# Kept sums of weights made in DRAM by adding transfers instead of on VectorE

## The chip, the cores and the metric

One core of one Trainium2 chip. The time is the device time of one execution in microseconds, the median of some runs. A core has five engines that run their own instruction streams in order and wait for each other through semaphores: TensorE (PE; its weight loads are shown as PEld), VectorE (DVE), ScalarE (ACT), GpSimd (POOL) and SyncE (SP), which here only issues transfers. 16 DMA engines serve the transfers that SP, ACT and POOL issue.

## The reference

Two layers over 256 tokens of width 2048, float32. Layer 0 mixes tokens by neighbourhood attention (16 heads), layer 1 by a gated short convolution; each is followed by a gated MLP (width 5632) with a convolution over three positions. Cut to what matters:

```python
for i in range(2):
    a = rms_norm(h, mix_norm[i])
    mixed = (neighborhood_attention(a, na_w_qkv[0], na_rpb[0], na_w_o[0]) if i == 0 else
             short_conv_mixer(a, sc_w_in[0], sc_conv_w[0], sc_w_out[0]))
    h = h + mixed
    h = h + conv_glu_ffn(rms_norm(h, ffn_norm[i]), ffn_w_up[i], ffn_conv_w[i], ffn_conv_b[i], ffn_w_down[i])
return rms_norm(h, final_norm)
# conv_glu_ffn: [g, u] = dwconv3(x @ w_up) + b;  (silu(g) * u) @ w_down
```

## The kernel before

Every float32 matrix product is split: a weight tile (`raw`, one chunk of 8 x 128 columns, 512 KB) is cast by ScalarE to a short part `hi` (line 185), VectorE subtracts to get the rest `lo` (line 188), and TensorE multiplies hi x both parts of the activations and lo x their high part. There are six `raw`, six `hi` and six `lo` buffers; SP may load a chunk when the subtraction that read the buffer's old content is over.

Two kinds of products follow each other. A `Phase` (QK, up projections, short-conv input; lines 262 and 270) gives features on partitions; an item of it is two output tiles of four chunks in all. `Tokens` (attention output, down projections, short-conv output; lines 463 to 465) gives tokens on partitions. For certain pairs of contraction tiles, marked H in the plans, `Tokens` uses a Strassen-like form with seven products in place of eight (`seven`, line 467). It needs sums of weight blocks. With l, r and t for the left block, the right block of the same rows and the right block of the next, these are l+r, t+r and l+r+t, 256 KB each. They are made long before, while another product runs, and kept in DRAM: this is the "kept" tensor, one per marked pair and half of the columns, 64 in all. One such making is a job.

The job is written by `make`. It takes three tiles of the activation pool (`act_tile`), loads l, r and t into them through SP, and puts off two steps in the list `stores`: ADDS chunks later VectorE does three adds (lines 207 to 209), and STORES chunks later ScalarE issues three stores (line 214). `take` hands jobs to phases; a phase gives its jobs to the items from `hosts[0]` to `hosts[1]`. QK_JOBS, V_JOBS, UP_JOBS and SC_JOBS say how many jobs which phase gets: none in the last head group of the attention, 11, 10, 8 and 10 in the four up projections, 15 in the short-conv input.

The seven products need sums of activation blocks as well, the forms: `make_forms` adds them on GpSimd (lines 526 to 529) from two finished `conv` tiles, and `split_into` (lines 301 and 302, ScalarE and VectorE) splits them in two parts at once.

The order of instructions on each engine is fixed when the program is built, by a scheduler that follows the program's order and `issue_after` edges. `tick` counts places in an item's run; `after(n, fn)` puts a step off by n ticks.

In the attention, four head groups alternate between a `Phase` for queries and keys and `Values` (lines 689 to 691). Scores, softmax and its transposes are strewn into them: VectorE scales the scores and adds the bias (line 624; GpSimd added a mask to the bias before, line 603), finds the maximum (627) and, after the exponential on ScalarE (629), normalises (632); TensorE transposes the result (642) into a PSUM tile that has one buffer, and ScalarE and VectorE split that (301, 302).

Of the kernel before, what the change touches and what calls it, by code (L numbers as in the profile page):

```python
# [15 lines left out]
F32 = mybir.dt.float32  # L16
F32R = mybir.dt.float32r
AF = mybir.ActivationFunctionType
ALU = mybir.AluOpType
# [3 lines left out]
P = 128  # L23
# [35 lines left out]
QK_JOBS, V_JOBS, UP_JOBS, SC_JOBS = (0, 2, 2, 0), (2, 2, 2, 0), (11, 10, 8, 10), 15  # L59
# [12 lines left out]
C_END = C_ID + P  # L72

LEAD = 96
ADDS, STORES = 1, 3
RAWS = 6


# [1 line left out]
def trunk(ctx, tc, xT, par, bias, wqk, wv, wo, wsc, wscout, wup, wdown, out):  # L80
    nc = tc.nc
# [48 lines left out]
    def prep_to(n):  # L130
        while len(prepped) < min(n, len(chunks)):
            src, w, kind = chunks[len(prepped)]
            for due in [x for x in stores if x[0] <= len(prepped)]:
                stores.remove(due)
                due[1]()
            if kind == "make":
                make(*src)
                prepped.append(())
                continue
            raw = wp.tile([P, CH * P], F32, name="raw", tag="raw", bufs=RAWS)  # L140
            if kind == "rows":
                load(raw[:, :w], src)
                prepped.append(parts(raw[:, :w]) + (raw,))
                continue

            if kind == "kept":
                t42, left, sums = prepped[-1][2], prepped[-2][2], src()
                load(t42[:, 4 * P:], sums[:, 8 * P:])
                load(raw, sums[:, :8 * P])
                nc.vector.tensor_add(out=t42[:, :4 * P].rearrange("p (f c) -> p f c", f=4),  # L150
                                     in0=t42[:, 4 * P:].rearrange("p (f c) -> p f c", f=4),
                                     in1=left.rearrange("p (f k c) -> p k f c", f=4, c=P)[:, 1])
                prepped.append((parts(raw), parts(t42)))
                continue

            load(raw[:, :4 * w].rearrange("p (f c) -> p f c", f=4), src.rearrange("f p c -> p f c"))
            prepped.append(parts(raw[:, :4 * w].rearrange("p (f k c) -> p f k c", f=4, c=P)) + (raw,))

    def load(out, in_, strict=True):

        with ExitStack() as order:
            if "SP" in newest:
                order.enter_context(tc.issue_after(newest["SP"].ins))
            last = nc.sync.dma_start(out=out, in_=in_)
        if strict:
            newest["SP"] = last
# [23 lines left out]

    kept, newest, fenced = {}, {}, []

    def make(w, g, i, sets, strict):

        kept[id(w), g, i] = dst = dp.tile([P, 3, 4 * P], F32, name=f"kept{len(kept)}")
        if len(sets) < 2:
            sets.append([act_tile().bitcast(F32) for _ in range(3)])
        else:
            sets.reverse()
        for x, f, k in zip(sets[-1], (0, 4, 4), (0, 0, 1)):  # L200
            f, k = 8 * g + f, 2 * i + k
            load(x.rearrange("p (f c) -> p f c", f=4), w[f:f + 4, :, k * P:(k + 1) * P].rearrange("f p c -> p f c"), strict)
        l, r, t = sets[-1]

        def adds():
            with tc.issue_after(newest["DVE"].ins):
                nc.vector.tensor_add(out=l, in0=l, in1=r)
                nc.vector.tensor_add(out=r, in0=t, in1=r)
                nc.vector.tensor_add(out=t, in0=l, in1=t)

        def store():
            for n, x in enumerate((l, r, t)):
                with tc.issue_after(newest["ACT"].ins):
                    nc.scalar.dma_start(out=dst[:, n], in_=x)
        stores.append((len(prepped) + ADDS, adds))
        stores.append((len(prepped) + STORES, store))

    jobs = []
# [1 line left out]
    def plan_jobs(w, plans):  # L220
        jobs.extend((w, g, i) for g, (order, sset, _) in enumerate(plans) for i in order if i in sset)

    def take(n, strict=True):
        sets = []
        out, jobs[:] = [(*job, sets, strict) for job in jobs[:n]], jobs[n:]
        return out

    class Phase:
# [52 lines left out]
    def after(n, fn):  # L281
        later.append((at[0] + n, fn))

    item = [0]
    at = [0]
# [9 lines left out]
    def split_into(hi, lo, src):  # L295

        with ExitStack() as order:
            if fenced:
                for x in ("ACT", "DVE"):
                    order.enter_context(tc.issue_after(newest[x].ins))  # L300
            first = nc.scalar.copy(out=hi, in_=src)  # L301
            nc.vector.tensor_sub(out=lo, in0=src, in1=hi.bitcast(F32))  # L302
        return first
# [9 lines left out]
    def act_tile():  # L313
        return ap_.tile([P, 2 * S], F32R, name="act", tag="act", bufs=HALF)
# [194 lines left out]
    def form_slots(blocks):  # L509

        if not form_at:
            return [left_over.pop() for _ in range(3)]
        tag = next(x for x in form_at if blocks == 3 or x != "sf")
        form_at.remove(tag)
        y = tp.tile([P, (6 if tag == "sf" else 8) * P], F32R, name="sf", tag=tag)
        if tag != "sf" and blocks == 3:
            left_over.append(y[:, 6 * P:])
        return y

    def make_forms(xe, xo, place, fresh=False):  # L520

        if fresh:
            form_at[:], left_over[:] = ("sf", "vv", "qk") * 2, ()
        v = tp.tile([P, 4, P], F32, name="s", tag="s")
        x11, x21, x12, x22 = (x[:, t * P:(t + 1) * P] for x in (xe, xo) for t in range(2))
        nc.gpsimd.tensor_sub(out=v[:, 0, :], in0=x21, in1=x22)
        nc.gpsimd.tensor_sub(out=v[:, 1, :], in0=v[:, 0, :], in1=x11)
        nc.gpsimd.tensor_add(out=v[:, 3, :], in0=x12, in1=v[:, 1, :])
        nc.gpsimd.tensor_sub(out=v[:, 2, :], in0=x11, in1=x21)  # L529
        if isinstance(place, tuple):  # L530
            hi, lo = place
            split_into(hi, lo, v.rearrange("p f c -> p (f c)"))
            return [(hi[:, j * P:(j + 1) * P], lo[:, j * P:(j + 1) * P]) for j in (0, 1, 3, 2)]

        blocks = 3 if place else 4
        y = form_slots(blocks)
        if isinstance(y, list):
            for j in range(3):
                split_into(y[j][:, :P], y[j][:, P:], v[:, j])
            at = [(x[:, :P], x[:, P:]) for x in y]  # L540
        else:
            y = y.rearrange("p (b t c) -> p t b c", t=2, c=P)
            split_into(y[:, 0, :blocks], y[:, 1, :blocks], v[:, :blocks])
            at = [(y[:, 0, j], y[:, 1, j]) for j in range(blocks)]
        if place:
            at.append((place[:, P:2 * P], place[:, 3 * P:]))
            split_into(*at[3], v[:, 3])
        return [at[j] for j in (0, 1, 3, 2)]

    def in_both(plans, i):  # L550
# [2 lines left out]
    def to_norm(n, a):  # L553

        ssq = ep.tile([P, 2, KT // 4], F32, name=f"ssq{n}")

        def evac(t, q, ps):
            added = residual(t, q, ps)
            squares(t, q, ssq)

            def next_input():
                for k0, tag in zip(range(4 * q - 4, 4 * q + 4, 2), ("tr", "o", "sc", "st")):
                    tr = transposed(k0, tag)
                    for k in range(2):
                        a[k0 + k] = a_tile()
                        scaled_split(a[k0 + k], tr[:, k, :], norm_g(n, k0 + k))
            if t and q % 2:
                after(1, next_input)
                if q == KT // 4 - 1:
                    after(2, lambda: spread_factor(token_factor(ssq)[0]))  # L570
            return added
        return evac


    a0 = [None] * KT
# [284 lines left out]
        plan_jobs(down[1, half], S_MLP[1, half])  # L860
    for g in range(NH // 4):
        Phase(wqk, range(8 * g, 8 * g + 8), KT, a0, qk_evac, intro=0 if g else INTRO, step=STEP,
              jobs=take(QK_JOBS[g], False), hosts=(0, 4))
        Values(g, a0, take(V_JOBS[g], False))
    Tokens(wo, KT, oT, to_norm(1, a1), S_ATT, oforms)
    mlp(0, a1, to_norm(2, a2))
    Phase(wsc, range(3 * KT), KT, a2, sc_evac, intro=3, jobs=take(SC_JOBS), hosts=(8, 29))
# [36 lines left out]
    for r in range(KT // STEP):  # L904
        for i in range(STEP // 2):
            k = r * STEP + 2 * i
# [12 lines left out]
    for item[0], (ph, ft, c, k0, ka, kb) in enumerate(items):  # L919

        with ExitStack() as order:
# [4 lines left out]
            if item[0] != KT // STEP * INTRO:  # L926
# [3 lines left out]
                end, n = ends[item[0]], FURTHER if getattr(ph, "fence", False) else AHEAD  # L930
# [77 lines left out]
```

## Time and profile before

| | before |
|---|---|
| median of 3 runs, us | 2202.33 (2196.28 to 2202.39) |
| profiled execution, us | 2200.65 |
| its span, us | 2198.8 |
| PE, PEld busy, us | 2181.2, 1890.9 |
| DVE, ACT, POOL busy, us | 1847.5, 1305.4, 118.5 |
| three adds of the jobs (L207, L208, L209), us | 44.4, 44.6, 45.5, x64 each |
| stores of the jobs (L214) | 192 of 256 KB, 4.8 us to landing |
| DMA in all | 555.34 MB, mean 253 GB/s |
| HBM read, written | 500.70 MB, 52.43 MB |

Busy times are unions over the span. Matmuls are pipelined and overlap: the mean time of one (391 ns for a 128x512 product) is longer than the distance at which they follow each other. In the tables of windows each row is a stretch of the span; a PE that is busy for the whole stretch at clock 1.00 cannot be made faster by any other engine there.

### The profile page before, as it was taken

The page shows a single profiled execution, that of the slowest core. Times are in us where ns is not written, and L with a number is a line of the kernel's source. Part 1 is how long each engine was busy: PE and PEld are TensorE (multiplying, and loading weights), DVE is VectorE, ACT ScalarE, POOL GpSimd, SP SyncE. Part 2 cuts the span into 40 slices and gives each one's busy share as a digit, 9 for nine tenths or more (in the row PEclk, how much of TensorE's full clock was granted, in tenths as well). Part 3 has the DMA queues.
Part 4 walks back from the last instruction along what each step waited for, and adds up shares of the span by engine and source line. Part 5 has one row for each costly group of instructions (what it writes and reads, how often), then busy time and mean ns, then how long its engine had stood idle before and what let it go on. Part 6 is the DMA issues. An engine that isn't in the chain of part 4 may idle for free.

```text
span 2198.8 us, 33369 instructions
## 1 busy us (share of the span) xinstructions
PE 2181.2 (99%) x11716; PEld 1890.9 (86%) x11716; DVE 1847.5 (84%) x2842; ACT 1305.4 (59%) x1985; POOL 118.5 (5%) x155
## 2 busy tenths in 40 slices
PE   9999999999999999999999999999999999999998
PEld 8888888888888888888888888888888888888886
DVE  8787677888988889988888777888898898898787
ACT  7555556666655656665665555565666665666565
POOL 1010000001100000100000100000010000000000
PEclk9999999999999999999999999999999999999999
DMA  8687656789858879866878888776976787897575
GB/s 302 223 294 229 222 166 212 229 275 315 272 182 268 275 254 317 293 208 216 268 250 290 291 292 291 234 240 221 302 262 198 230 274 253 295 311 242 177 259 173
DMA packets 362072, 555.34 MB, mean 253 GB/s; under 512 B 21680, under 2 KB 249136, under 8 KB 361904
## 3 DMA queue, kind: packets, MB, share of 16 engines
q1 hardware_dynamic: 332880, 502.23, 70.0%
q10 hardware_dynamic: 29024, 50.98, 6.1%
q8 instruction: 92, 1.51, 0.3%
q14 instruction: 76, 0.62, 0.1%
HBM read 500.70 MB, written 52.43 MB: 252 GB/s over the span
## 4 chain that ended last, share of the span: by engine, by line
PE 96%; DVE 1%; DMA 1%; issue 1%; SPq 0%; ACT 0%; DVEq 0%
PE mm L262 42%; PE mm L270 22%; PE mm L465 7%; PE mm L463 7%; PE mm L464 7%; PE mu L463 3%; PE mu L465 3%; PE mu L464 3%; PE mm L690 1%; PE mm L689 1%; PE mm L691 1%; DMA act<-in_wdown 1%; PE tr L371 1%; DMA bias<-in_bias 0%; DVE lo L188 0%
## 5 line engine op out<-in xcount | busy, mean ns | idle before, releaser
L185 ACT CAST hi<-raw 128x1024 fp32r<-128x1024 f32 (+1 forms) x920 | 917.6, 1012 | 372.6 <-PE mm L465 128.6
L188 DVE TENSOR_TENSOR lo<-raw,hi 128x1024 fp32r<-128x1024 f32 (+1 forms) x856 | 1020.1, 1215 | 141.1 <-ACT hi L185 66.1
L262 PE MATMUL mm<-a,hi 128*128 128x512 f32 x4096 | 963.1, 391 | 0.3 <-DVE a L310 0.2
L262 PEld LDWEIGHTS mm<-a,hi 128*128 128x128 f32 x4096 | 758.8, 188 | 152.4 <-DVE a L310 1.3
L270 PEld LDWEIGHTS mm<-a,lo 128*128 128x128 f32 x4096 | 514.0, 191 | 12.5
L270 PE MATMUL mm<-a,lo 128*128 128x256 f32 x4096 | 519.4, 283 | 0.0
L463 PE MATMUL mm<-hi,act 128*128 128x512 f32 x634 | 247.3, 390 | 0.0
L465 PE MATMUL mm<-hi,act 128*128 128x512 f32 x634 | 246.7, 389 | 0.0
L464 PE MATMUL mm<-lo,act 128*128 128x512 f32 x576 | 224.4, 390 | 0.0
L341 DVE SCALAR_TENSOR_TENSOR conv<-pad,pt,conv 128x256 f32<-128x256 f32 x384 | 181.2, 484 | 19.1 <-ACT conv L339 13.4
L325 ACT COPY corr<-mm 128x256 f32<-128x256 f32 x256 | 92.6, 370 | 174.9 <-PE mm L270 171.3
L339 ACT ACTIVATE conv<-pad,pt 128x256 f32<-128x256 f32 x176 | 104.1, 600 | 153.9 <-DVE pad L331 139.4
L465 PEld LDWEIGHTS mm<-hi,act 128*128 128x128 f32 x634 | 119.0, 188 | 24.7
L463 PEld LDWEIGHTS mm<-hi,act 128*128 128x128 f32 x634 | 119.1, 188 | 24.4 <-DVE h L360 0.2
L464 PEld LDWEIGHTS mm<-lo,act 128*128 128x128 f32 x576 | 108.2, 188 | 22.0
L326 DVE TENSOR_TENSOR corr<-mm,corr 128x256 f32<-128x256 f32 x256 | 106.7, 420 | 17.4 <-ACT corr L325 16.6
L529 POOL TENSOR_TENSOR s<-conv 128x128 f32<-128x128 f32 x27 | 29.3, 1085 | 993.5 <-DVE conv L748 993.5
L302 DVE TENSOR_TENSOR act<-conv,act 128x256 fp32r<-128x256 f32 x88 | 39.0, 443 | 48.2 <-ACT act L301 48.0
L331 DVE TENSOR_TENSOR pad<-corr,rstd 128x256 f32<-128x256 f32 x176 | 73.2, 424 | 0.3
L463 PE MATMUL mu<-hi,sf 128*128 128x512 f32 x180 | 70.0, 389 | 0.0
L464 PE MATMUL mu<-lo,sf 128*128 128x512 f32 x180 | 70.0, 389 | 0.0
L465 PE MATMUL mu<-hi,sf 128*128 128x512 f32 x180 | 70.0, 389 | 0.0
(160 smaller groups left out, 1594.1 us busy)
## 6 DMA issues: line engine op xcount, KB each, us to landing
raw<-in_wup SPq DMA_DIRECT2D x352, 512.0 KB, 5.3
raw<-in_wdown SPq DMA_DIRECT2D x124, 512.0 KB, 4.9
kept<-act ACTq DMA_DIRECT2D x192, 256.0 KB, 4.8
raw<-in_wsc SPq DMA_DIRECT2D x96, 512.0 KB, 5.4
act<-in_wdown SPq DMA_DIRECT2D x156, 256.0 KB, 6.0
raw<-kept SPq DMA_DIRECT2D x64, 512.0 KB, 4.9
raw<-in_wqk SPq DMA_DIRECT2D x56, 512.0 KB, 5.4
raw<-in_wv SPq DMA_DIRECT2D x32, 512.0 KB, 4.5
```

The source lines that it names most:

```text
L185: newest["ACT"] = nc.scalar.copy(out=hv, in_=r)
L188: newest["DVE"] = nc.vector.tensor_sub(out=lv, in0=r, in1=hv.bitcast(F32))
L262: nc.tensor.matmul(self.ps[ft], lhsT=prepped[i][0][:, o:o + P], rhs=self.src[k], start=k == 0, stop=False)
L270: nc.tensor.matmul(self.ps[ft][:, S:], lhsT=prepped[i][1][:, o:o + P], rhs=self.src[k][:, :S], start=False, stop=k == self.nk - 1)
L325: nc.scalar.copy(out=corr, in_=ps[:, S:])
L326: nc.vector.tensor_add(out=corr, in0=ps[:, :S], in1=corr)
L331: nc.vector.tensor_mul(out=dst, in0=both(ps), in1=rstd)
L339: nc.scalar.activation(c, x[:, 1:S + 1], AF.Identity, scale=w[1], bias=b)
L341: nc.vector.scalar_tensor_tensor(out=c, in0=x[:, tap:tap + S], scalar=w[tap], in1=c, op0=ALU.mult, op1=ALU.add)
L463: nc.tensor.matmul(ps, lhsT=xh, rhs=wh, start=start, stop=False)
L464: nc.tensor.matmul(ps, lhsT=xh, rhs=wl, start=False, stop=False)
L465: nc.tensor.matmul(ps, lhsT=xl, rhs=wh, start=False, stop=stop)
```

## The change

The three tiles of activations are no longer used by a job. SP copies l, t and t straight into the kept tensor, DRAM to DRAM. After that GpSimd issues transfers that add to what is there (`accum_op`): r to the first piece, r to the second, and, when the first has landed, the first piece to the third. The first two stand ADDS = 2 chunks after the copies, the third STORES = 5 chunks. Neither VectorE nor ScalarE has a part in a job. `strict`, which ordered a job's loads among the others on SP, is gone: all of them are loads that later ones need not follow. And `make_forms` no longer splits at once: where it made its own tiles the splits come LATE = 4 ticks later. Lines from 215 on move up by a few.

```diff
-ADDS, STORES = 1, 3
+ADDS, STORES = 2, 5
+LATE = 4
...
-    def make(w, g, i, sets, strict):
+    def make(w, g, i):
 
         kept[id(w), g, i] = dst = dp.tile([P, 3, 4 * P], F32, name=f"kept{len(kept)}")
-        if len(sets) < 2:
-            sets.append([act_tile().bitcast(F32) for _ in range(3)])
-        else:
-            sets.reverse()
-        for x, f, k in zip(sets[-1], (0, 4, 4), (0, 0, 1)):
-            f, k = 8 * g + f, 2 * i + k
-            load(x.rearrange("p (f c) -> p f c", f=4), w[f:f + 4, :, k * P:(k + 1) * P].rearrange("f p c -> p f c"), strict)
-        l, r, t = sets[-1]
+        l, r, t = (w[8 * g + f:8 * g + f + 4, :, (2 * i + k) * P:(2 * i + k + 1) * P].rearrange("f p c -> p f c")
+                   for f, k in ((0, 0), (4, 0), (4, 1)))
+        at = [dst[:, n].rearrange("p (f c) -> p f c", f=4) for n in range(3)]
+        for n, x in ((0, l), (1, t), (2, t)):
+            load(at[n], x, False)
 
         def adds():
-            with tc.issue_after(newest["DVE"].ins):
-                nc.vector.tensor_add(out=l, in0=l, in1=r)
-                nc.vector.tensor_add(out=r, in0=t, in1=r)
-                nc.vector.tensor_add(out=t, in0=l, in1=t)
+            nc.gpsimd.dma_start(out=at[0], in_=r, accum_op=ALU.add)
+            nc.gpsimd.dma_start(out=at[1], in_=r, accum_op=ALU.add)
 
         def store():
-            for n, x in enumerate((l, r, t)):
-                with tc.issue_after(newest["ACT"].ins):
-                    nc.scalar.dma_start(out=dst[:, n], in_=x)
+            nc.gpsimd.dma_start(out=at[2], in_=at[0], accum_op=ALU.add)
         stores.append((len(prepped) + ADDS, adds))
         stores.append((len(prepped) + STORES, store))
...
-    def take(n, strict=True):
-        sets = []
-        out, jobs[:] = [(*job, sets, strict) for job in jobs[:n]], jobs[n:]
+    def take(n):
+        out, jobs[:] = jobs[:n], jobs[n:]
         return out
...
         if isinstance(y, list):
-            for j in range(3):
-                split_into(y[j][:, :P], y[j][:, P:], v[:, j])
             at = [(x[:, :P], x[:, P:]) for x in y]
+            to = [(*at[j], v[:, j]) for j in range(3)]
         else:
             y = y.rearrange("p (b t c) -> p t b c", t=2, c=P)
-            split_into(y[:, 0, :blocks], y[:, 1, :blocks], v[:, :blocks])
             at = [(y[:, 0, j], y[:, 1, j]) for j in range(blocks)]
+            to = [(y[:, 0, :blocks], y[:, 1, :blocks], v[:, :blocks])]
         if place:
             at.append((place[:, P:2 * P], place[:, 3 * P:]))
-            split_into(*at[3], v[:, 3])
+            to.append((*at[3], v[:, 3]))
+
+        def splits():
+            for x in to:
+                split_into(*x)
+        after(LATE, splits)
```

How the order of instructions moves is shown at three places. The first is VectorE in the values of head group 0, from the scaling of one head's scores (`s_835`, then `s_831`) to the splits of the first transposed tile (`tr_879`, then `tr_866`). Before:

```order
L207 TENSOR_TENSOR act_864<-act_864,act_865 128x512
L302 TENSOR_TENSOR qk_765<-qk_763,qk_765 128x256
L595 TENSOR_TENSOR qk_790<-corr_787,rstd_82 128x256
L208 TENSOR_TENSOR act_865<-act_866,act_865 128x512
L624 SCALAR_TENSOR_TENSOR s_835<-sc_828,bias_624 128x256
...
L302 TENSOR_TENSOR act_884<-tr_879,act_884 128x256
L188 TENSOR_TENSOR lo_905<-raw_902,hi_904 128x1024
L630 RECIPROCAL z_837<-z_837 128x2
L188 TENSOR_TENSOR lo_926<-raw_923,hi_925 128x1024
L632 TENSOR_SCALAR s_835<-s_835,z_837 128x256 x2
L302 TENSOR_TENSOR act_885<-tr_879,act_885 128x256
```

Now:

```order
L189 TENSOR_TENSOR lo_895<-raw_892,hi_894 128x1024
L621 SCALAR_TENSOR_TENSOR s_831<-sc_824,bias_624 128x256
L295 TENSOR_TENSOR qk_765<-qk_790,qk_765 128x256
L621 SCALAR_TENSOR_TENSOR s_831<-sc_824,bias_624 128x256
L295 TENSOR_TENSOR act_871<-tr_866,act_871 128x256
L624 TENSOR_REDUCE m_832<-s_831 128x2
L295 TENSOR_TENSOR act_872<-tr_866,act_872 128x256
```

The adds are gone, and the two splits of the transposed tile stand on both sides of the reduction, with no conversion (`lo`) between them. On TensorE the second set of transposes of this group stands ten products earlier than before; in groups 1 and 2 the transposes keep their places.

The second is VectorE in group 1, between the normalisations of two heads. Before:

```order
L632 TENSOR_SCALAR s_1590<-s_1590,z_1592 128x256 x2
L207 TENSOR_TENSOR act_1637<-act_1637,act_1638 128x512
L188 TENSOR_TENSOR lo_1706<-raw_1703,hi_1705 128x1024
L208 TENSOR_TENSOR act_1638<-act_1639,act_1638 128x512
L207 TENSOR_TENSOR act_1676<-act_1676,act_1677 128x512
L209 TENSOR_TENSOR act_1639<-act_1637,act_1639 128x512
L208 TENSOR_TENSOR act_1677<-act_1678,act_1677 128x512
```

Of these the change keeps the normalisation and the conversion (`lo`); the adds have no successor on VectorE.

The third is GpSimd in the same part, where `bias` is the bias of a head. Before:

```order
L603 TENSOR_TENSOR bias_1293<-bias_1293,pt_79 128x384
L603 TENSOR_TENSOR bias_1419<-bias_1419,pt_79 128x384
L603 TENSOR_TENSOR bias_1569<-bias_1569,pt_79 128x384
```

Now:

```order
L600 TENSOR_TENSOR bias_1401<-bias_1401,pt_79 128x384
L204 DMA kept4_1612<-in_wdown 128x4x128
L205 DMA kept4_1612<-in_wdown 128x4x128
L208 DMA kept4_1612<-kept4_1612 128x512
L204 DMA kept5_1644<-in_wdown 128x4x128
L205 DMA kept5_1644<-in_wdown 128x4x128
L208 DMA kept5_1644<-kept5_1644 128x512
L600 TENSOR_TENSOR bias_1544<-bias_1544,pt_79 128x384
```

The adding transfers of two jobs now stand between the bias additions of two heads, and the third transfer of a job directly behind the two that it follows.

More of the change, by code (lines that the diff above doesn't have):

```diff
@@ L862, in trunk @@
         Phase(wqk, range(8 * g, 8 * g + 8), KT, a0, qk_evac, intro=0 if g else INTRO, step=STEP,
-              jobs=take(QK_JOBS[g], False), hosts=(0, 4))
-        Values(g, a0, take(V_JOBS[g], False))
+              jobs=take(QK_JOBS[g]), hosts=(0, 4))
+        Values(g, a0, take(V_JOBS[g]))
     Tokens(wo, KT, oT, to_norm(1, a1), S_ATT, oforms)
```

## The prediction

> **What bounds the kernel now.** I read the busy times first, then the same engines in 40 windows of 55 us, then TensorE's own waits, and last VectorE's timeline round those waits.
>
> ```profile
> PE 2181.2 (99%) x11716; PEld 1890.9 (86%) x11716; DVE 1847.5 (84%) x2842; ACT 1305.4 (59%) x1985; POOL 118.5 (5%) x155
> ```
>
> ```profile
> 275.00:330.00 55.00, 55.00 (x298) 47.47 (x297) 39.40 (x65) 28.56 (x53) 5.21 (x9) 1.00 0.52 166
> ...
> 2090.00:2145.00 55.00, 55.00 (x252) 45.80 (x251) 46.92 (x55) 35.68 (x46) 0.00 (x0) 1.00 0.78 258
> ```
>
> The window rows hold start and end, the length, the busy time of PE, PEld, DVE, ACT and POOL, then TensorE's granted clock, the DMA engines' share and GB/s. From 275 to 2145 us each window has PE busy for 55.00 of its 55 us at clock 1.00; the first and last of them stand here. In there nothing that VectorE or ScalarE is spared can shorten the run; a delay of the weights can lengthen it. What can be won lies before 275 us or in the tail, and the change does not touch the tail.
>
> ```profile
> PE tr L642 <- DVE s L632: 4.5, 3, 2.0
> PE tr L642 <- DVE act L302: 2.9, 1, 2.9
> ```
>
> ```profile
> 66.50:76.50 10.00, 7.10 (x30) 5.64 (x29) 9.91 (x16) 4.41 (x9) 0.99 (x1) 0.83 0.78 250
> 150.00:160.00 10.00, 8.11 (x38) 6.46 (x37) 9.56 (x12) 5.02 (x10) 3.69 (x2) 1.00 1.04 349
> 228.00:238.00 10.00, 7.41 (x28) 5.71 (x27) 8.55 (x11) 4.43 (x9) 2.10 (x2) 0.83 0.98 344
> 290.00:315.00 25.00, 25.00 (x124) 21.04 (x123) 18.53 (x33) 12.76 (x25) 0.00 (x0) 1.00 0.64 209
> ```
>
> All of TensorE's real waits in the attention are for the transposes of the softmax (L642). They fall in the value products of head groups 0, 1 and 2, one per group: 10.00 - 7.10 = 2.90, 1.89 and 2.59 us idle. Group 3 (last row) has none. Groups 0 to 2 carry sums to be kept, group 3 carries none (V_JOBS ends in 0). Two of the three also cost clock: 0.83 over 10 us is 1.7 us of full speed lost.
>
> **Part 1: the adds leave VectorE.** Here are the pieces of its timeline between two normalisations (L632) in group 1, and the same piece in group 3.
>
> ```profile
> 140.80 0.61 DVE L632 TENSOR_SCALAR s<-s,z 128x256 f32<-128x256 f32 x2
> 143.26 0.69 DVE L207 TENSOR_TENSOR act<-act 128x512 f32<-128x512 f32 x1 [1.85 <-DMA act<-in_wdown]
> ...
> 155.30 1.34 DVE L632 TENSOR_SCALAR s<-s,z 128x256 f32<-128x256 f32 x2
> ...
> 220.12 0.69 DVE L207 TENSOR_TENSOR act<-act 128x512 f32<-128x512 f32 x1 [2.42 <-DMA act<-in_wdown]
> ...
> 294.91 0.61 DVE L632 TENSOR_SCALAR s<-s,z 128x256 f32<-128x256 f32 x2
> ...
> 303.37 0.62 DVE L632 TENSOR_SCALAR s<-s,z 128x256 f32<-128x256 f32 x2
> ```
>
> From one to the next it is 14.5 us in group 1 (140.80 to 155.30) and 8.5 us in group 3. The 6.0 us between them are a wait of 1.85 us for the job's load, and six adds of 0.7 us (the first is the row at 143.26): 1.85 + 4.2 = 6.05. TensorE waited 1.89 us at the end of it, so with the adds gone 4 us are to spare. Group 2 is the same with a wait of 2.42: 6.6 us are taken out, 2.59 are needed. In group 0 six adds (4.2 us) go, and two more things move. The second split of the first head's probabilities stands two conversions earlier on VectorE, and TensorE's second set of transposes stands ten products earlier (10 x 0.23 = 2.3 us), so 2.90 + 2.3 = 5.2 us are needed. The adds give 4.2, and the two conversions and the normalisation that the split no longer stands behind give
>
> ```profile
> 67.27 1.22 DVE L188 TENSOR_TENSOR lo<-raw,hi 128x1024 fp32r<-128x1024 f32 x1
> ...
> 70.90 0.41 DVE L302 TENSOR_TENSOR act<-tr,act 128x256 fp32r<-128x256 f32 x1
> ```
>
> 3.6 us (67.27 to 70.90): 7.8 against 5.2. All three stalls should go: 2.90 + 1.89 + 2.59 = 7.4 us, and the two stretches of lower clock, which follow a stall each, with them: 2 x 1.7 = 3.4 us. **Gain 10.8 us.** The rest of the 192 adds (135 us of VectorE), and the 192 stores that ScalarE no longer issues, lie under a TensorE that is busy throughout: worth 0 there. They do buy margin for what Part 2 costs.
>
> **Part 2: the same sums by transfers.** This part can only cost. A job moves six pieces of 256 KB now (three loads, three stores), 1.57 MB. The windows give what the DMA engines carry:
>
> ```profile
> 495.00:550.00 55.00, 55.00 (x317) 48.65 (x317) 48.49 (x84) 33.45 (x56) 10.01 (x11) 1.00 0.94 315
> 550.00:605.00 55.00, 55.00 (x317) 48.64 (x316) 50.28 (x87) 34.40 (x59) 7.36 (x8) 1.00 0.81 269
> 605.00:660.00 55.00, 55.00 (x311) 48.34 (x310) 46.97 (x79) 32.70 (x55) 2.12 (x4) 1.00 0.57 182
> 1210.00:1265.00 55.00, 55.00 (x318) 48.69 (x317) 43.59 (x71) 27.89 (x39) 5.84 (x4) 1.00 0.89 292
> ```
>
> ```profile
> q10 hardware_dynamic: 29024, 50.98, 6.1%
> ```
>
> 315 GB/s at a share of 0.94 make 335 GB/s when full. A job so costs 1.57 MB / 335 GB/s = 4.7 us of all 16 engines. Writing to DRAM is no dearer than loading (q10, nearly all of it the stores: 50.98 MB in 6.1% of 2198.8 us, 380 GB/s), so the three DRAM-to-DRAM copies keep the price of the three loads, 2.35 us. The three adding transfers are not in the trace. Their floor is that of a store, 2.35 us, and then nothing changes. I take twice, 4.7 us, since each must read what it adds to beside what it adds, and the reading row is the nearest. As the upper end I take three times, 7.0 us, if writing is not overlapped with the two reads. The Trainium skill ("Collectives: The Full Stack", on why a reduce-scatter is half of an all-gather) says that an add inside a transfer needs two source reads and measured a ratio of 1.93; no adding transfer runs in this trace, and by that figure, an estimate, they would take 4.5 us.
>
> In the up projections of the first MLP 11 jobs fall on 14 items:
>
> ```profile
> 506.59 7.28 PE mm L262 x32
> 513.87 3.83 PE mm L270 x32
> ```
>
> One item is 11.11 us, so a job comes every 14.1 us, 3.9 in a window. At twice, 3.9 x 2.35 = 9.2 us are added to a window of 55, 0.17: 0.94 becomes 1.11, 0.81 becomes 0.98, 0.57 has room. The first window falls 0.06 to 0.11 behind (150:160 above ran at 1.04), 3.3 to 6 us. The short-conv projection (1210:1265) has 15 jobs on 21 items (233 us, one job in 15.5) and goes from 0.89 to 0.89 + 2.35 / 15.5 = 1.04, 9 us behind at its end. How late may a weight be? One chunk of the up projection:
>
> ```profile
> 522.50 1.04 ACT L185 CAST hi<-raw 128x1024 fp32r<-128x1024 f32 x1
> ...
> 528.65 7.44 PE L262 MATMUL mm<-a,hi 128*128 128x512 f32 x32
> ```
>
> It has landed when ScalarE converts it, from 522.50 to 523.54, and it is the third of the four chunks in the row at 528.65 (1.82 us each, 7.28 / 4), read at 528.65 + 2 x 1.82 = 532.3. So it may come 8.8 us late. 3.3 to 6 us fit in, 9 us just about: **cost 0, up to about 2 us**. At the floor price the cost is 0.
>
> **Part 3: later splits** (LATE). They move the small casts and subtractions of the forms four ticks back; the forms are read in the next token product only, and no wait of TensorE in the rows above is for them. Cost 0. What the delay covers is GpSimd, which now waits for landings ahead of the forms; the last rival prices it when the cover is gone.
>
> **The sum.** The profiled execution took 2200.65 us with its span of 2198.8. 2200.65 - 10.8 + 1 (half of the 2 us above) = 2190.9. The median of the runs shown, 2202.33, is 1.7 above the profiled one and the lowest, 2196.28, 4.4 below it, so I leave it there: **2191 us**, own range 2186 to 2196.
>
> **The rivals.**
>
> *A new wait for the old one.* The bias add of each head stands on GpSimd, and now behind the adding transfers of the jobs: the third waits until the first has landed.
>
> ```profile
> raw<-in_wup SPq DMA_DIRECT2D x352, 512.0 KB, 5.3
> ...
> act<-in_wdown SPq DMA_DIRECT2D x156, 256.0 KB, 6.0
> ```
>
> ```profile
> 131.88 1.04 POOL L603 TENSOR_TENSOR bias<-bias,pt 128x384 f32<-128x384 f32 x1 [12.59 <-DMA bias<-in_bias]
> ...
> 148.35 0.42 DVE L624 SCALAR_TENSOR_TENSOR s<-sc,bias 128x256 f32<-128x256 f32 x1
> ```
>
> In group 1 that add runs at 131.88 and is wanted at 148.35, 15.4 us after its end. One landing as long as the job loads (6.0) ends at 138, two in a row at 144. If one takes over 15 us, VectorE waits for the bias and the transposes are late again. Then 7 to 10 of the 10.8 us come back: 2198 to 2201. For it: in groups 1 and 2 two jobs stand in a row on GpSimd. Against it: the margin is twice the landing. Together with a price of the adding transfers between twice and three times, which eats the gain, chance 0.22.
>
> *Weights late (slower).* If an adding transfer costs three times a store, a job adds 4.7 us, a window 18.3 us, 0.33. The first up window then needs 1.27, the next 1.14: 15 + 8 us behind, less the 8.8 us of lead and what the 0.57 window gives back, some 12 us of TensorE per up projection. Four of them, the third with 8 jobs, make about 43 us. Short conv gets + 4.7 / 15.5 = 0.30, and (0.89 + 0.30 - 1) x 233 - 9 = 35 us. 2191 + 78 = 2269 us. It decides from about 2.3 times, where 0.94 + 0.22 outgrows the lead. For it: pieces of 512 bytes land slowest (6.0 us for 256 KB beside 5.3 for 512 KB). Against it: the 0.57 window and the idle DMA of the token products. Chance 0.20.
>
> *GpSimd falls behind (slower).* If issue and landing of one job's sums take over 14.1 us, the forms queue behind them, the conv tiles that they read come free late, and ScalarE stops at L339. With issue and landing at 16 us it is 2 us for each of 54 jobs, 108, less about 9 us of lead in each of five projections: 2191 + 60 = 2250 us. Chance 0.08.
>
> **How the numbers follow.** Forecast 0.50, the wait that comes back 0.22, the two slow ones 0.28. 0.3% (6.6 us) is about what a measurement of this kernel can tell from no change. The forecast lies at -0.5% and counts as faster; the wait that comes back counts as the same; the others as slower. The range goes from 2186 (all 10.8 us and a run as low as the lowest) to 2225 (weights late at some 2.5 times). Above it lie the full prices of the slow cases, 0.2 together.
>
> **What would show it.** Right: no wait at L642 in the attention, clock 1.00 from 5 us on, PE 55.00 of 55 up to 2145, the end some 11 us earlier. The DMA share above 1.0 at 495:550 without a PE gap shows twice the price. Wrong: PE waits for hi (L185) or lo (L188) inside the projections (weights late), GpSimd waiting for its own transfers ahead of a bias add (the wait that comes back), or ScalarE at L339 waiting for GpSimd.

## The result, and the profile after

The changed kernel takes 2233.07 us (median of 4 runs, 2231.67 to 2235.14) beside 2200.73 for the kernel before on the same chip: 1.0151 times as long, 95% interval 1.0133 to 1.0169. It is 1.5% slower; the forecast was 2191.

The busy times and the DMA queues of the changed kernel (its span is 2229.9 us), from the first and third parts of its page:

```profile
PE 2193.6 (98%) x11716; PEld 1900.0 (85%) x11716; DVE 1737.6 (78%) x2650; ACT 1286.3 (58%) x1985; POOL 308.2 (14%) x347
...
q1 hardware_dynamic: 332880, 502.23, 68.6%
q0 software_dynamic: 76800, 50.34, 17.1%
```

VectorE has 110 us less to do, as intended, and TensorE 12.4 us more, for the same products; most of that is time at a lower clock (the mean granted clock is 0.992, 0.997 before: 0.8% of 2229.9 less 0.3% of 2198.8 is 11.2 us). q0 holds the adding transfers. Windows, with the columns as in the prediction: the three of the attention, and four in the up projections:

```profile
66.50:76.50 10.00, 5.48 (x20) 4.25 (x19) 9.57 (x15) 4.55 (x11) 1.89 (x3) 0.83 1.06 286
150.00:160.00 10.00, 10.00 (x47) 8.28 (x47) 6.12 (x8) 4.64 (x9) 2.55 (x2) 1.00 1.13 319
228.00:238.00 10.00, 10.00 (x48) 8.26 (x47) 5.38 (x7) 5.08 (x8) 1.83 (x1) 1.00 0.66 220
495.00:550.00 55.00, 51.15 (x279) 44.49 (x278) 35.09 (x61) 26.35 (x44) 15.97 (x19) 0.97 0.99 258
550.00:605.00 55.00, 48.57 (x265) 42.63 (x264) 39.00 (x66) 26.63 (x45) 13.97 (x17) 0.94 0.94 241
880.00:945.00 65.00, 57.60 (x309) 50.59 (x308) 44.74 (x75) 33.10 (x55) 20.14 (x25) 0.92 1.03 251
1960.00:1975.00 15.00, 12.63 (x65) 11.19 (x64) 9.14 (x16) 7.30 (x13) 6.11 (x8) 0.89 1.11 231
```

In the attention, groups 1 and 2 (second and third row) are as forecast: no idle time, full clock. Group 0 (first row) is worse, 4.52 us idle for 2.90. The loss lies in the last four rows, in projections where TensorE had no gap at all before. What it waits for there, and who waits one step further back, stands in the view of waits (sum, how often, longest, in us):

```profile
POOL kept L208 <- DMA kept<-in_wdown: 292.5, 48, 8.7
DVE sf L295 <- ACT sf L294: 113.9, 26, 11.3
ACT sf L294 <- POOL s L520: 102.7, 24, 11.2
ACT hi L186 <- DMA raw<-in_wup: 26.9, 29, 2.8
PE mm L263 <- DVE lo L189: 20.9, 8, 5.2
PE tr L639 <- DVE act L295: 4.5, 1, 4.5
```

Read from the last row but one upwards: eight waits of TensorE for the low part of a weight; VectorE, which makes it, waits for ScalarE at the split of a form (`sf`), and ScalarE for GpSimd's form (`s`). Before, that last wait was 22.7 us in 19 and no longer than 1.9. The weights of the up projections are not late: ScalarE's wait for `raw<-in_wup` was 31.1 us before. Those of the short-conv input are later (31.2 us for `raw<-in_wsc`, 8.2 before), but the one gap of TensorE in that projection, 0.83 us, stands behind a form too. GpSimd at last waits 292.5 us at L208, the third adding transfer of a job, for the first to land. The longest of the gaps by the timeline, GpSimd, then ScalarE, then TensorE:

```profile
578.42 1.28 POOL L204 DMA_DIRECT2D kept<-in_wdown  x1 [2.87 <-DMA kept<-in_wdown]
579.19 1.78 POOL L205 DMA_DIRECT2D kept<-in_wdown  x1
587.38 0.87 POOL L208 DMA_DIRECT2D kept<-kept  x1 [6.42 <-DMA kept<-in_wdown]
587.95 0.78 POOL L519 TENSOR_TENSOR s<-conv 128x128 f32<-128x128 f32 x1
588.81 0.45 POOL L520 TENSOR_TENSOR s<-s,conv 128x128 f32<-128x128 f32 x1
...
582.65 0.40 ACT L294 CAST act<-conv 128x256 fp32r<-128x256 f32 x1
589.29 0.51 ACT L294 CAST sf<-s 128x384 fp32r<-128x384 f32 x1 [6.24 <-POOL s L520]
590.03 1.04 ACT L186 CAST hi<-raw 128x1024 fp32r<-128x1024 f32 x1
...
591.79 1.44 PE L263 MATMUL mm<-a,lo 128*128 128x256 f32 x5 [5.24 <-DVE lo L189]
```

ScalarE split the second of the two `conv` tiles at 582.65, so both were there. GpSimd stood at L208 until 587.38 and made the form only then; ScalarE stood at the form's split for 6.24 us with the next weight conversion (590.03) behind it, and TensorE ran dry. The reason that this could happen is in the order of ScalarE's instructions. Around the split of the first form of an up projection, before the change and after it:

```
before                                      after
L301 CAST act_4671<-conv_4666 128x256       L294 CAST act_4607<-conv_4602 128x256
L301 CAST sf_4679<-s_4674 128x3x128         L294 CAST sf_4615<-s_4610 128x3x128
L301 CAST act_4549<-s_4674 128x128          L294 CAST act_4489<-s_4610 128x128
L185 CAST hi_4711<-raw_4709 128x1024        L186 CAST hi_4762<-raw_4760 128x1024
```

The form's split stands directly behind the activation's split in both. LATE = 4 has put nothing off: the splits are now called from `tick`, where `fenced` is empty (only while something is in that list does a split get an `issue_after` edge behind the newest weight conversion), so they carry no such edge, and the scheduler places them as early as before. Among the 30 forms of this kind there is none with a weight conversion in between.

### The profile page after: what moved, and what is told of

Read it like the earlier page. It is cut to its first block, busy times and chain, and to the rows that moved or that the text cites. A ratio compares the mean times of both kernels' runs of the same rounds, so it can differ in the third digit from the quotient of the medians.

```text
span 2229.9 us, 33099 instructions
## 1 busy us (share of the span) xinstructions
PE 2193.6 (98%) x11716; PEld 1900.0 (85%) x11716; DVE 1737.6 (78%) x2650; ACT 1286.3 (58%) x1985; POOL 308.2 (14%) x347
## 3 DMA queue, kind: packets, MB, share of 16 engines
q0 software_dynamic: 76800, 50.34, 17.1%
## 4 chain that ended last, share of the span: by engine, by line
PE 79%; DMA 10%; DVE 5%; ACT 3%; issue 2%; POOL 1%; SPq 0%; DVEq 0%; ACTq 0%; POOLq 0%
PE mm L255 30%; PE mm L263 16%; DMA kept<-in_wdown 9%; PE mm L456 6%; PE mm L458 6%; PE mm L457 6%; PE mu L456 3%; PE mu L458 3%; PE mu L457 3%; DVE lo L189 2%; ACT hi L186 1%; PE mm L686 1%; PE mm L688 1%; PE mm L687 1%; PE tr L364 1%
## 5 line engine op out<-in xcount | busy, mean ns | idle before, releaser
L263 PE MATMUL mm<-a,lo 128*128 128x256 f32 x4096 | 526.7, 285 | 20.9 <-DVE lo L189 20.9
L204 POOL DMA_DIRECT2D kept<-in_wdown x52 | 67.5, 1297 | 672.3 <-DMA kept<-in_wdown 671.9
L318 ACT COPY corr<-mm 128x256 f32<-128x256 f32 x256 | 85.9, 368 | 60.2 <-PE mm L263 59.8
L208 POOL DMA_DIRECT2D kept<-kept x64 | 54.8, 855 | 400.9 <-DMA kept<-in_wdown 292.5
L295 DVE TENSOR_TENSOR sf<-s,sf 128x384 fp32r<-128x384 f32 (+2 forms) x37 | 19.1, 522 | 114.0 <-ACT sf L294 113.9
L205 POOL DMA_DIRECT2D kept<-in_wdown x52 | 82.2, 1580 | 8.0 <-DMA kept<-in_wdown 7.0
L294 ACT CAST sf<-s 128x384 fp32r<-128x384 f32 (+2 forms) x37 | 17.2, 466 | 111.6 <-POOL s L520 102.7
```

The source lines that it names most:

```text
L205: nc.gpsimd.dma_start(out=at[1], in_=r, accum_op=ALU.add)
L263: nc.tensor.matmul(self.ps[ft][:, S:], lhsT=prepped[i][1][:, o:o + P], rhs=self.src[k][:, :S], start=False, stop=k == self.nk - 1)
L318: nc.scalar.copy(out=corr, in_=ps[:, S:])
```

## The experiments

The theory after this reading: GpSimd's forms stand behind a transfer that waits for a landing, and ScalarE waits for the form with the weights behind it (*forms late*). The rival is the one that the prediction feared most: the adding transfers take the DMA engines from the weights (*weights late*).

### The splits really later

```diff
-LATE = 4
+LATE = 8
...
         def splits():
+            fenced.append(True)
             for x in to:
                 split_into(*x)
+            fenced.clear()
```

> The changed kernel, but the split of a form is ordered behind the newest weight conversion on ScalarE when it is written, with LATE = 8: it then stands five conversions (some 14 us) behind the split of the activation, where the changed kernel, in spite of LATE = 4, has it directly behind that split (0 conversions later, in all 30 forms). Theory (forms late): GpSimd's forms stand behind an adding transfer that waits for a landing, and ScalarE, in order, waits for the form with the weights behind it; its waits there are 102.7 us in 24, the longest 11.2. With 14 us in hand these end: the 30 us lost in the projections come back, 2197 to 2205 us. Rival (weights late): the adding transfers take the DMA engines from the weights; then the place of the split changes nothing, 2228 to 2238 us.

Measured: 2196.3 us, 0.9981 of before (0.9972 to 0.9991). Its busy times, DMA queue, waits and two windows:

```profile
PE 2179.1 (99%) x11716; PEld 1890.6 (86%) x11716; DVE 1748.6 (80%) x2650; ACT 1312.3 (60%) x1985; POOL 328.1 (15%) x347
...
q0 software_dynamic: 76800, 50.34, 16.9%
```

```profile
POOL kept L208 <- DMA kept<-in_wdown: 341.9, 51, 8.2
ACT hi L186 <- DMA raw<-in_wup: 32.0, 35, 2.8
PE tr L641 <- DVE act L295: 4.4, 1, 4.4
```

```profile
495.00:550.00 55.00, 55.00 (x319) 48.76 (x318) 46.44 (x73) 33.04 (x53) 22.19 (x24) 1.00 1.14 302
550.00:605.00 55.00, 55.00 (x319) 48.75 (x318) 45.19 (x76) 34.43 (x56) 8.58 (x13) 1.00 0.84 244
```

GpSimd waits even longer for its landings (341.9 us), the DMA engines carry the same bytes in less time, and TensorE has no gap in any projection. ScalarE's waits for GpSimd's forms in the up projections are gone, and so is the whole loss: of the 35.7 us between the two spans (2229.9 and 2194.2), 14.5 are TensorE's busy time (2193.6 - 2179.1, the lower clock) and 21.2 its idle time. *Weights late* falls for the projections.

### The transfers behind the forms

```diff
-ADDS, STORES = 2, 5
+ADDS, STORES = 4, 12
...
+            with ExitStack() as order:
+                if "POOL" in newest:
+                    order.enter_context(tc.issue_after(newest["POOL"].ins))
+                ... (the two adding transfers; the same around the third)
...
-        nc.gpsimd.tensor_sub(out=v[:, 2, :], in0=x11, in1=x21)
+        newest["POOL"] = nc.gpsimd.tensor_sub(out=v[:, 2, :], in0=x11, in1=x21)
```

The edges are needed: with STORES at 8, 12 or 18 alone, GpSimd's list of instructions in the built program has the same order as with 5 (these programs were not run). Nothing but data tied the transfers to a place.

> The changed kernel, but each adding transfer is ordered behind the newest form on GpSimd, ADDS, STORES = 4, 12. The transfers and their bytes stay the same, and so does the place of the splits. Theory (forms late): forms no longer stand behind a transfer that waits for a landing; ScalarE's waits for GpSimd shrink from 102.7 us to under 40, and the time falls to 2198 to 2210 us. Rival (weights late): the same load on the DMA engines, 2228 to 2238 us.

Measured: 2202.81 us, 1.0012 of before (1.0003 to 1.0021). Waits (lines 294, 520 and 263 are 300, 526 and 269 in it):

```profile
ACT sf L300 <- POOL s L526: 66.9, 17, 14.6
PE mm L269 <- DVE lo L189: 3.4, 2, 2.8
```

The time is in the range of *forms late*, and far from the rival's. ScalarE's waits did not fall under 40 us as expected; but only two of them still reach TensorE, with 3.4 us in place of 20.9. What counts is when a wait falls, not their sum.

### LATE = 0

```diff
-LATE = 4
+LATE = 0
```

> The changed kernel with LATE = 0, which undoes the later splits alone. The order of the form splits among ScalarE's weight conversions is the same as with LATE = 4 (0 conversions behind the activation's split in all 30). Theory (the delay was never in the order): the same time, 2229 to 2237 us. Rival (the delay covers part of GpSimd's wait): slower, above 2245 us.

Measured: 2228.94 us, 1.0131 of before (1.0111 to 1.0152), the end of its interval inside that of the change (1.0133 to 1.0169), from two runs and 0.1 us below the range. ScalarE's waits for forms (99.2 us in 26) and the eight of TensorE for `lo` (20.3 us) are as with LATE = 4, which so covered nothing, as the order of instructions says. Of the 4.1 us by which the median is lower, 1.5 lie in group 0 and come below; the rest I have not traced.

### One conversion in between

The splits ordered as in the first experiment, but with LATE = 4, which puts each of them one weight conversion back, not five.

```diff
         def splits():
+            fenced.append(True)
             for x in to:
                 split_into(*x)
+            fenced.clear()
```

> The changed kernel with the split of each form ordered behind the newest conversion, LATE = 4: it then stands one conversion behind the activation's split, not five. One chunk is 2.78 us of TensorE (a quarter of an item of 11.11). Theory (the form is late by a fixed time and what stands behind its split waits as long): each of the eight waits in the projections shrinks by about 2.8 us, so that of 2.07, 1.79, 1.19, 5.24, 3.54, 3.86, 0.83 and 2.37 (20.9 us) 2.5 + 0.8 + 1.1 = 4.3 stay, with most of the lower clock gone; 2203 to 2210 us. Rival (it is the order relative to the activation's split, not the time): all waits go, 2195 to 2199, or none does, 2228 to 2238 us.

Measured: 2201.09 us, 1.0005 of before (0.9996 to 1.0015), 2 us under the range. Waits:

```profile
ACT sf L294 <- POOL s L520: 71.6, 15, 5.8
PE mm L255 <- DVE corr L319: 2.8, 2, 1.9
```

The eight waits for `lo` are gone. What is left of ScalarE's wait reaches TensorE in other places: twice through `corr`, 2.8 us, once at the start of a token product (0.5 us). One conversion of lead brings back 32.0 of the 36.8 us that five bring (2233.07 to 2201.09, and to 2196.3), where I had left 4.3 us of waits and some lower clock. That a delay of one conversion is enough for most, and five for all, fits a form that is late by a few us.

### Which wait on GpSimd

```diff
-            nc.gpsimd.dma_start(out=at[2], in_=at[0], accum_op=ALU.add)
+            nc.gpsimd.dma_start(out=at[2], in_=l, accum_op=ALU.add)
```

> The changed kernel, but the third adding transfer of a job adds the left block from the input in place of the first sum: it leaves the right block out of that sum, and need not wait until the first has landed. Bytes, transfers and the order on GpSimd stay (its source is read in pieces of 512 bytes and not 2 KB). If the wait for that landing (292.5 us in 48 in the projections of the MLPs) is what holds the forms: GpSimd's waits at the third go, ScalarE's waits for forms fall from 102.7 to under 30 us, 2196 to 2204 us. If the wait for the copies ahead of the first two (L204), or GpSimd's time to issue (0.9 to 1.6 us each), holds them: 2215 to 2232 us.

Measured: 2197.11 us, 0.9985 of before (0.9976 to 0.9994). Waits:

```profile
POOL kept L204 <- DMA kept<-in_wdown: 871.8, 50, 146.1
ACT sf L294 <- POOL s L520: 14.2, 19, 5.4
POOL kept L208 <- DMA kept<-in_wdown: 9.9, 12, 1.8
```

With three adding transfers of the same size in the same order, but none that needs another's landing, ScalarE's waits fall from 102.7 to 14.2 us. GpSimd's waits ahead of a job's first transfer grow to 871.8 us and do no harm (the longest, 146.1 us, is the pause between two projections). So it was the wait for the landing at L208, not the wait for the copies and not the time to issue. Nor was it the load on the DMA engines: the third transfer, which now reads pieces of 512 bytes, makes the queue dearer (18.6% of the engines, 17.1% in the changed kernel).

### The adding itself

```diff
-            nc.gpsimd.dma_start(out=at[0], in_=r, accum_op=ALU.add)
+            nc.gpsimd.dma_start(out=at[0], in_=r)
... (the other two likewise)
```

> The changed kernel, but GpSimd's three transfers of a job copy and do not add: the sums are left out, so the kept tensors hold wrong values; bytes written, queues, waits and order are the same. If adding costs a transfer nothing beside a copy: GpSimd's queue stays at 17 % of the DMA engines and the time at 2228 to 2238 us. If an adding transfer costs 2.8 times a store (17.1 % against 6.1 %): the queue falls to 6 or 7 %, landing from 10.0 us to 6 or 7, and GpSimd waits some 3 us less at each third transfer. Theory (forms late): ScalarE's waits for the forms (102.7 us) fall to 40 to 60, 2208 to 2220 us. Rival (weights late): the whole loss goes, 2196 to 2202 us.

Measured: 2191.28 us, 0.9961 of before (0.9946 to 0.9976). The queue and two waits:

```profile
q0 software_dynamic: 15360, 50.34, 6.7%
...
POOL kept L208 <- DMA kept<-in_wdown: 235.0, 51, 6.7
ACT sf L294 <- POOL s L520: 28.2, 18, 3.2
```

The median landing of the first two transfers of a job (52 jobs), by the sixth part of the pages, with the adding first and then without:

```profile
kept<-in_wdown POOLq DMA_DIRECT2D x104, 256.0 KB, 10.0
```

```profile
kept<-in_wdown POOLq DMA_DIRECT2D x104, 256.0 KB, 6.5
```

The third lands sooner in both (7.1 and 5.4 us). This gives the price: 17.1% of 2229.9 us is 381 us for 64 jobs, 6.0 each; 6.7% of 2189.7 is 147, 2.3 each. An adding transfer takes 2.6 times the DMA time of a plain one. The time fits neither range. By itself the run can't part the theories, since it makes landings shorter and frees the DMA engines at once. It was wrong to expect that ScalarE's waits, halved or quartered, would still cost half: none of them is over 3.2 us now, and such waits TensorE does not see (the kernel before had 19 up to 1.9). The wait of group 0 is nearly gone too (1.0 us), which the next runs take up.

### The attention

Four runs ask where the gain and the loss of the attention come from. In the first, the kernel before keeps its adds on VectorE in the projections and its splits as they were; the ten jobs of the attention alone use the changed `make`:

```diff
 (kernel before)
         kept[id(w), g, i] = dst = dp.tile([P, 3, 4 * P], F32, name=f"kept{len(kept)}")
+        if not strict:
+            ... (copies, two adding transfers after 2 chunks, the third after 5)
+            return
```

> The kernel before, with the ten jobs of the attention alone made by copies and adding transfers; the 54 jobs in the projections stay with VectorE, and the splits of the forms are as before. Theory (the adds on VectorE were what held the softmax in groups 1 and 2): the waits of 1.89 and 2.59 us go, with 1.7 us of clock, the one of group 0 grows to about 4.5; 2200.3 - 6.2 + 1.6 = 2195 to 2197.5 us, and the projections have no wait. Rival (the gain of the attention came from the later splits or is not there without them): 2199 to 2202 us.

Measured: 2196.03 us, 0.9981 of before (0.9971 to 0.9990). Windows of groups 0, 1 and 2:

```profile
66.50:76.50 10.00, 5.68 (x23) 4.56 (x22) 9.33 (x16) 4.86 (x12) 2.53 (x3) 0.83 1.05 286
150.00:160.00 10.00, 10.00 (x48) 8.26 (x47) 7.08 (x10) 5.33 (x10) 2.55 (x2) 1.00 1.09 304
228.00:238.00 10.00, 10.00 (x48) 8.28 (x47) 6.24 (x7) 5.74 (x8) 1.01 (x1) 1.00 0.54 187
```

The gain of groups 1 and 2 is there without any change to the splits, and so is the wait of 4.3 us in group 0. Most of the latter can be followed in ScalarE's timeline of the changed kernel, where the exponential of the softmax (62.00) stands behind two weight conversions that wait for their loads:

```profile
58.17 1.05 ACT L186 CAST hi<-raw 128x1024 fp32r<-128x1024 f32 x1 [4.90 <-DMA raw<-in_wv]
61.05 1.05 ACT L186 CAST hi<-raw 128x1024 fp32r<-128x1024 f32 x1 [1.82 <-DMA raw<-in_wv]
62.00 0.51 ACT L626 ACTIVATE s<-s,m 128x256 f32<-128x256 f32 x1
```

Before, the same conversions waited 1.65 and 0.41 us. Between 30 and 62 us the median landing of the weights is 6.7 us for `raw<-in_wv` and 10.3 for `raw<-in_wqk`, 5.7 and 5.4 before. About 1.5 us of the 4.5 has another source, again on GpSimd:

```profile
67.90 0.85 POOL L208 DMA_DIRECT2D kept<-kept  x1 [9.69 <-DMA kept<-in_wo]
68.47 1.30 POOL L600 TENSOR_TENSOR bias<-bias,pt 128x384 f32<-128x384 f32 x1
...
68.18 1.88 DVE L295 TENSOR_TENSOR qk<-qk 128x256 fp32r<-128x256 f32 x1
```

A bias add that has stood behind a third adding transfer runs beside a subtraction of VectorE, and that takes 1.88 us, where the one before it, of the same size and kind, takes 0.41 (at 66.04). In the LATE = 0 run the two do not meet, the subtraction takes 0.41, and TensorE's wait is 3.00 us, not 4.52. The next run removes both sources at once. It takes the splits-later kernel and moves the two jobs of group 0 to group 3, which had none:

```diff
-QK_JOBS, V_JOBS, UP_JOBS, SC_JOBS = (0, 2, 2, 0), (2, 2, 2, 0), (11, 10, 8, 10), 15
+QK_JOBS, V_JOBS, UP_JOBS, SC_JOBS = (0, 2, 2, 0), (0, 2, 2, 2), (11, 10, 8, 10), 15
```

> The kernel with the splits five conversions later (2196.3 us), and its two jobs of the first head group moved to the last (V_JOBS 0, 2, 2, 2). What is left of TensorE's waits there is one of 4.4 us for the transposes at 70.8 us, with 1.7 us of clock. Theory (the weights come late in group 0: ScalarE waits 4.90 and 1.82 us for its chunks at 53 to 61 us, and the softmax stands behind them): without the jobs the wait goes or falls under 1 us, 2189 to 2192 us, and nothing new appears in group 3, which had no jobs. Rival (the wait belongs to the order of the softmax itself, as the 2.90 us before): it stays, 2194 to 2198 us.

Measured: 2190.13 us, 0.9954 of before (0.9942 to 0.9967). Window of group 0:

```profile
66.50:76.50 10.00, 10.00 (x53) 8.40 (x52) 7.70 (x15) 5.02 (x10) 4.73 (x3) 1.00 1.01 298
```

The wait is gone, and TensorE has no gap from 14.4 us to the tail. This version beats both kernels. The same line changed in the kernel with transfers in the attention alone:

> The kernel with adding transfers for the ten jobs of the attention alone (2196.0 us), and its two jobs of the first head group moved to the last. The wait of 4.3 us at 71 us and 1.7 us of clock should go, as they did with all jobs made by transfers (2196.3 to 2190.1): 2189 to 2191.5 us. If so, transfers instead of adds are worth nothing in the projections. Rival (VectorE's or ScalarE's spared time in the projections gains something): 2192.5 us or more, above the 2190.1 of the kernel that makes all jobs by transfers.

Measured: 2190.05 us, 0.9954 of before (0.9942 to 0.9966), 0.1 us from the run above. So in the projections, transfers in place of the adds are worth nothing: ten of the 64 jobs carry the whole gain. And the same line changed in the kernel before, with all adds on VectorE:

> The kernel before, adds on VectorE, with only the two jobs of the first head group moved to the last. Theory (three adds and a wait for the load in each job hold the softmax wherever they stand): the wait of 2.90 us in group 0 and its 1.7 us of clock go, one of 1.9 to 2.6 us, with up to 1.7 us of clock, comes in group 3; 2196 to 2200 us. Rival (the adds cost in group 0 alone, or the last group has room): 2191 to 2196 us.

Measured: 2196.53 us, 0.9985 of before (0.9976 to 0.9993). All of TensorE's waits for VectorE at the transposes, and windows of groups 1 and 2:

```profile
PE tr L642 <- DVE s L632: 5.3, 2, 3.2
...
150.00:160.00 10.00, 7.93 (x38) 6.26 (x37) 8.08 (x10) 4.52 (x7) 1.94 (x2) 1.00 0.88 310
228.00:238.00 10.00, 7.86 (x30) 6.56 (x31) 6.62 (x9) 2.69 (x6) 1.52 (x1) 0.83 0.79 288
```

The time lies in the lower part of the first range, just above the rival's. The trace decides for the second half of the rival, that the last group has room: the wait of group 0 is gone and none comes in group 3. But the adds do cost in groups 1 and 2 (2.06 and 3.20 us here; the second wait begins before the window of its row), so they hold the softmax there, though not wherever they stand. Why group 3 has room was not tried.

## Why the prediction was wrong

*Bound, and Part 1 for groups 1 and 2: right.* Both waits went, and the run with transfers in the attention alone shows that nothing else is needed.

*Part 1 for group 0: wrong.* The working set 7.8 us of VectorE against a need of 5.2, and took the weights as on time there. ScalarE waited 4.66 us longer for them (4.90 + 1.82 - 1.65 - 0.41), ahead of the exponential, and a subtraction on VectorE took 1.5 us longer beside a late bias add. Term: a gain of 2.9 + 1.7 us, measured as a loss of 1.6; moving the two jobs wins the 6.2 us between (2196.3 to 2190.1).

*Part 2, the price: too low, and yet harmless in the projections.* Three adding transfers cost a job 6.0 us of the DMA engines, not 4.7; the floor of 2.35 was met by plain copies (2.3). The share foreseen for the first two windows of the up projection was 1.11 and 0.98; the splits-later kernel, where TensorE runs freely, shows 1.14 and 0.84. The lead of the weights was enough, as argued. But the rival built on it put the point of decision at 2.3 times, and at 2.6 no weight was late enough to stop TensorE in a projection of that kernel: its chance of 0.20 rested on a limit that was too near. It happened in group 0 instead, where I had not looked for it. The Trainium skill ("Collectives: The Full Stack", on why a reduce-scatter is half of an all-gather) has a ratio of 1.93; here it is 2.6, in 76,800 packets for the bytes that plain copies move in 15,360, so the measurement decides. The rival's "pieces of 512 bytes land slowest" is not general either: in the kernel before, 256 KB loads of `raw<-in_wdown` in such pieces land in 4.1 us, beside 4.9 for 512 KB of the same tensor.

*Part 3: this is the step that failed.* "They move the small casts and subtractions of the forms four ticks back", and "What the delay covers is GpSimd, which now waits for landings ahead of the forms", cost 0. Nothing was moved, and GpSimd's wait reached TensorE. I took the effect of LATE from the code and did not look it up in ScalarE's order, where it can be seen before any run. With the cover believed in, the forms' place behind the third adding transfer looked free. Undoing that (the splits really later) brings back 36.8 us (2233.07 to 2196.3), and the two jobs of group 0 moved another 6.2 (to 2190.1): together 42.9, where forecast and result are 42.1 apart.

*The rivals.* The wait for the bias did not come: no wait at the transposes of groups 1 and 2. "GpSimd falls behind" was the right engine with the wrong condition, place and price. It asked for issue and landing of over 14.1 us for each job, a stop at L339 through the conv tiles, and gave 2250. In fact a landing of 10.0 us was enough, since a form needs only to stand behind one such wait; the stop was at L294, and the cost 36.8 us. Of the signs named beforehand, waits of TensorE for `lo` inside the projections came, but I had put them down to weights that come late; the row of ScalarE's waits one step back (forms, not `raw`) tells the two apart.

## What to carry to other kernels

When an in-order engine is given a transfer that waits for another's landing, price what stands behind it on that engine by the full landing under load, and follow the chain through the next in-order engines up to the bound one. Where a scheduler orders the instructions, a postponement written in the program is worth nothing until it is seen in the list of instructions; an ordering edge made it real here. And work that only frees an engine off the critical path should be moved only where that engine holds something: ten of 64 jobs gave the whole gain.

## What was not expected of the hardware

An adding transfer is cut into pieces: 50.34 MB in 76,800 packets (655 bytes on average), where plain copies take 15,360 (3277 bytes). The count follows the pieces of the source: with the third transfer of a job reading pieces of 512 bytes in place of 2 KB it was 101,376. Under load the first two of a job land in 10.0 us, plain ones in 6.5. The Trainium skill ("DMA: Bandwidth & Descriptors", anatomy of a DMA on the GpSimd path) fits 2.0 us plus bytes over 436 GB/s for a single one, which would be 2.6 us for 256 KB, an estimate by that page; in this trace it is nearly four times as long. It was GpSimd's wait for it, not the DMA engines' load, that cost in the projections: the splits-later kernel moves the same bytes without the loss.

TensorE's clock falls after short gaps. Windows of the changed kernel around a gap of 2.07 us, one of 1.79 and one of 3.86:

```profile
510.00:520.00 10.00, 7.93 (x43) 6.97 (x42) 7.55 (x13) 4.60 (x9) 5.32 (x7) 0.83 1.00 182
536.00:546.00 10.00, 8.21 (x51) 7.20 (x50) 7.57 (x13) 4.62 (x9) 1.91 (x4) 1.00 0.63 173
...
932.00:942.00 10.00, 6.14 (x27) 5.55 (x26) 7.35 (x11) 3.95 (x7) 5.21 (x7) 0.67 1.03 194
```

0.83 over 10 us is 1.7 us lost, 0.67 is 3.3, nearly as much again as the gap. In group 0 of the changed kernel the 128x512 products right behind the gap of 4.52 us take 0.63 us, those before it 0.39. The length alone does not decide it: a gap of 2.06 us in the last run of the attention (150:160) left the clock at 1.00. The Trainium skill ("TensorE: Matmul & The Clock Gate", on oscillation in real kernels) warns of gaps over about 3.4 us; in these traces 2.07 us was once enough, so the measurement decides.
